# Block-group loads in the second expert pass: issued by ScalarE as two large DMAs instead of eight on SyncE, and gathers begun four rows ahead

## The chip, the cores and the metric

The kernel runs on one core of a Trainium2 chip. Its time is the device time of one execution in microseconds, the median of several runs. A profile is one further execution, taken by the hardware profiler.

## What is computed

The kernel is one step of a decoder layer for 512 prompt tokens and 64 sample tokens (width 2048, float32): a modulated norm, a combined input projection with a recurrent branch and a short convolution, an output projection, and then a layer of many tiny experts. Only this last layer matters here. Every token picks 16 of 16384 experts for each of 8 heads; an expert is one row of `u` and one row of `v`.

```
eidx = ...                                   # (token, head, 16): the experts picked, by product keys
g    = softmax(top)                          # their weights
act  = gelu(einsum('td,thkd->thk', x, u[eidx])) * g
out  = einsum('thk,thkd->td', act, v[eidx])
```

## The kernel before

The experts are 128 blocks of 128 rows. Blocks that are picked often are computed in full for all 512 prompt tokens, as dense matrix products: `L` = 88 of them. What the tokens pick in the other 40 blocks, and all picks of the sample tokens, is gathered row by row. The second half of the kernel is therefore two long passes on TensorE, with gathers woven between.

**The u part** runs over 88 blocks in two halves each (`NU2` = 176 halves, line 1492). `u_half` (line 1253) multiplies a half with the tokens; after the second half ScalarE takes the gelu and stores the block's activations to DRAM (`actd`, line 1267). In the meantime the matrix of weights, by block and token, is built in chunks and stored to DRAM as `gd` (line 1468).

**The v part** runs over `M` = 88 steps. A step takes four blocks (a "group", `SG` = 4, of which there are 22) and a quarter of the 2048 output columns, in four columns of 128 (`kq`, line 1596). `v_column` (line 1271) does 12 matmuls for a column, so a step has 48. Eight blocks, two groups, accumulate in PSUM over two steps; after the second, `v_sum` (line 1300) adds the bank to `acc` in SBUF: by ScalarE for the first eight blocks (line 1303), by VectorE after that (line 1305). Two buffers hold a bank of each kind, so that a late addition stops TensorE.

Both passes split every operand in two for precision. `ahead` (line 881) loads weights into `raw` on SyncE's queue (line 859 for u, 864 for v, two DMAs for each half) and converts them: ScalarE writes `xhi` (line 875), GpSimd `xlo` (line 876). A load waits until `xlo` has been made from the same buffer; a conversion waits until TensorE has used the buffer it writes. There are four buffers in the v part, and conversions run one step ahead.

Each group also needs its activations times its weights, split in two:

- `load_group(sg, j)` (line 1217) loads the group. It is called four times, with j = 0 to 3. Each call issues two DMAs on SyncE: the activations of one block (line 1223, 256 KB) and a quarter of the chunks of the weights `gd` (line 1224, 256 KB in runs of 512 B). The two tiles, `actr` and `gsb`, exist once.
- `weigh(sg)` (line 1227) multiplies them on VectorE, in `actr`'s place.
- `halve(sg, 0)` makes `ahi` on ScalarE (line 1237), `halve(sg, 1)` makes `alo` on VectorE (line 1241). After that `actr` is free for the next group.

When these are emitted is planned ahead: `jobs` (lines 1560 to 1572) maps a column's number (four a step) to calls. With `h_` the column of the first half of the split, and `hi_at` that of the group before, the four loads come at `hi_at + 5` to `hi_at + 8`, `weigh` at `h_ - 4`, the halves at `h_` and `h_ + 2`. The constraints in the loop make `h_` 16 columns, four steps, after `hi_at`. Groups 0 and 1 are loaded in the last 14 halves of the u part (from `E0`, lines 1539 to 1548).

**The gathers.** `gather_u` and `gather_v` (lines 1126 and 1160) append to two lists: `fetches` (an indirect DMA that GpSimd issues, line 1123, 128 rows of up to 8 KB into one row buffer) and `uses` (VectorE: a dot product at line 1151, or `accB += row * dots` at line 1177). `gather_to` (line 1206) walks through the uses in step with the columns, and before each use emits fetches up to a number of rows ahead. In the v part there are `RV` = 6 row buffers and the lead is `RV - 1` rows, the next use among them.

Every engine executes its instructions in the order in which this code emits them, and an instruction that waits for a semaphore holds all behind it.

Of the kernel before, what the change touches and what calls it, by code (L numbers as in the profile page):

```python
# [5 lines left out]
F32 = mybir.dt.float32  # L6
# [22 lines left out]
NA = NP  # L29
# [3 lines left out]
SG = 4  # L33
# [3 lines left out]
TC = 32  # L37
NCH = NA // TC
QT = NA // 128
SORTED = ((0, 64, 36), (64, 128, 43), (192, 128, 33), (320, 128, 27), (448, 64, 10))  # L40
RB = 4
RV = 6
# [32 lines left out]
def build(ctx, tc, A, O, dbg=None):  # L75
    nc = tc.nc
# [328 lines left out]
    o = big.tile([128, KD, T], F32, name="o", tag="big")  # L405

    def project(src, nm):
        his, los = stream_w(src, nm)
        p = pp.tile([128, 2, 512], F32, name=f"pp_{nm}", tag="pp")
        mm3([p[:, 0, :HT], p[:, 1, :HT]], his, los, movs)  # L410
        return p
# [185 lines left out]
    for k in range(KD):  # L597
        p = project(A["w_out"][k], f"o{k}")
# [32 lines left out]
    for q in range(4):  # L631
# [7 lines left out]
        t = adap.tile([128, 4, 512], F32, name=f"h2s{q}", tag="wa")  # L639
# [32 lines left out]
    gd = dr.tile([NCH, 128, L, TC], F32, name="gd")  # L672
    actd = dr.tile([L, 128, NA], F32, name="actd")
# [111 lines left out]
    slot_of, row_log, slots_now = {}, [], [RB]  # L785
# [8 lines left out]
    def row_free():  # L794

        s_ = (slot_of.get(len(row_log) - 1, -1) + 1) % slots_now[0]
        return all(row_log[k] for k in range(max(0, len(row_log) - 2 * RV), len(row_log)) if slot_of[k] == s_)
# [46 lines left out]
    raws, parts, gsb, ahl, acts, pools = {}, {}, {}, {}, {}, {}  # L844
# [36 lines left out]
    def ahead(l, c):  # L881
        while at["l"] <= min(l, len(stream) - 1):
            load(at["l"])
            at["l"] += 1
        while at["c"] <= min(c, len(stream) - 1):
            conv(at["c"])
            at["c"] += 1
# [73 lines left out]
    def sample_twice():  # L961

        for k0 in range(0, KD, 8):
            r, a = new_row(f"dup{k0}")
            row_log[a] = True
            d = r.bitcast(F32R).rearrange("p (q k t) -> p q k t", q=2, t=128)
            dups.append(d)
            for q in range(2):
                S.activation(d[:, q].rearrange("p k (r t) -> p k r t", t=NG),
                             r32(hv[q][:, k0:k0 + 8, None, NA:T]).to_broadcast([128, 8, 2, NG]), AF.Copy)  # L970

    def sample_rows():

        hT = first_h["h"] = psum["p"].tile([128, D], F32, name="hT0", tag="hT", bufs=1)
        for k in range(KD):
            for q in range(2):
                PE.matmul(hT[:, k * 128:(k + 1) * 128], dups[k // 8][:, q, k % 8, :], identr, start=q == 0, stop=q == 1)
# [134 lines left out]
    fetches, uses = [], []  # L1112
# [4 lines left out]
    def flush(n):  # L1117
        while after and after[0][0] <= n:
            after.pop(0)[1]()
# [84 lines left out]
    gf, gu = [0], [0]  # L1204

    def gather_to(n, lim=1 << 30):

        n = min(int(n), lim)
        while gu[0] < min(n, len(uses)):
            while gf[0] < min(len(fetches), gu[0] + (RB if slots_now[0] == RB else RV - 1), lim) and row_free():  # L1210
                fetches[gf[0]]()
                gf[0] += 1
            uses[gu[0]]()
            gu[0] += 1
            flush(gu[0])

    def load_group(sg, j):

        if j == 0:
            gsb[sg] = ep.tile([128, NCH, SG * TC], F32, name=f"gsb{sg}", tag="gsb", bufs=1)  # L1220
            acts[sg] = ep.tile([128, SG, NA], F32, name=f"actr{sg}", tag="actr", bufs=1)
        c = slice(j * NCH // 4, (j + 1) * NCH // 4)
        nc.sync.dma_start(acts[sg][:, j, :], actd[SG * sg + j])  # L1223
        nc.sync.dma_start(gsb[sg][:, c, :].rearrange("p c (i t) -> p c i t", t=TC),
                          gd[c, :, sg * SG:(sg + 1) * SG, :].rearrange("c p i t -> p c i t"))

    def weigh(sg):

        a = acts[sg].rearrange("p i (c t) -> p i c t", t=TC)
        V.tensor_tensor(a, a, gsb.pop(sg).rearrange("p c (i t) -> p i c t", t=TC), op=ALU.mult)  # L1230
# [195 lines left out]
    def g_start():  # L1426

        kb = pbank("g", "kb", 2)
        S.activation(kb[:, :L], perm[:, :L], AF.Copy)
        S.activation(kb[:, L:L + 128], iota, AF.Copy)  # L1430
        gk["w"], gk["o"] = kb[:, :L], kb[:, L:L + 128]
        gk["g"] = pbank("g", "gbank", 2)

    def g_pair(b):

        rg = pools["rg"]
        t0 = b * 4
        ops = rg.tile([128, 8, 128], F32, name=f"op{b}", tag="op", bufs=PAIRS // 2)
        wr = rg.tile([128, 8, L], F32, name=f"wr{b}", tag="wr", bufs=PAIRS // 2)
        for out, src, j in ((ops, gk["o"], 1), (wr, gk["w"], 0)):  # L1440
            n = src.shape[-1]
            V.tensor_tensor(out, src[:, None, :].to_broadcast([128, 8, n]),  # L1442
                            it[j][:, t0:t0 + 8, None].to_broadcast([128, 8, n]), op=ALU.is_equal)
        pair[b], pair[b + 1] = (ops, wr, 0), (ops, wr, 4)

    def g_scale(b):

        ops, wr, j0 = pair[b]
        for j in range(4):
            S.activation(ops[:, j0 + j, :], ops[:, j0 + j, :], AF.Copy, scale=it[2][:, b * 4 + j:b * 4 + j + 1])  # L1450
# [19 lines left out]
    def put(n):  # L1470
        for f in puts[:n]:
            f()
        del puts[:n]

    E0 = NU2 - 14
# [4 lines left out]
    ep = None  # L1480

    def upto(n):
        return min(NB2, max(0, (n - R1) * NB2 // (E0 - 6 - R1)))

    def g_one(n):
        nonlocal spare
        if gm[1] < min(upto(n - LAG), gm[2]):
            g_out(gm[1], g_mm(gm[1]))
            gm[1] += 1
            spare += 0.4  # L1490

    for n in range(NU2):
        _, i, c = stream[n]
        if n == 0:
            sample_twice()
        if n == 1:
            sample_rows()
        ahead(n + 3, n + 2)
        spare += PIECE
        if R1 is not None:  # L1500
            if not gk:
                g_start()
            put(2)
            g_one(n)
            if gm[0] < min(upto(n), gm[1] + PAIRS - 1):
                g_pair(gm[0])
                gm[0] += 2
                spare -= 2.2
            while gm[2] < min(gm[0], gm[1] + PAIRS - 2):
                g_scale(gm[2])  # L1510
                gm[2] += 1

        if R2 is None:
            due_g += RATE[R1 is not None] if ready[0] else 0
            g0 = gu[0]
            gather_to(due_g, ready[0])
            due_g = min(due_g, gu[0] + 1.0)
            spare -= 2.4 * (gu[0] - g0)
        else:
            gather_to(G0 + (NU + EARLY_V - G0) * (n + 1 - R2) // (NU2 - R2))  # L1520
        while spare > 0 and R2 is None:
            cost = next(steps1 if R1 is None else steps2, "end")
            if cost == "end":
                if R1 is None:
                    R1 = n
                else:
                    R2, G0 = n, gu[0]
                break
            if cost is None:
                break  # L1530
            spare -= cost
        if n == E0:
            assert not pair and not stg
            put(len(puts))
            p2.close()
            epx = ctx.enter_context(ExitStack())
            ep = epx.enter_context(tc.tile_pool(name="ep", bufs=1))
        u_half(n, i, c)
        for sg, o in ((0, 1), (1, 7)):
            if n - E0 in (o, o + 1):  # L1540
                load_group(sg, 2 * (n - E0 - o))
                load_group(sg, 2 * (n - E0 - o) + 1)
            if n - E0 == o + 3:
                weigh(sg)
            if n - E0 == o + 4:
                halve(sg, 0)
            if n - E0 == o + 5:
                halve(sg, 1)
    hp_.close()
    vp = ctx.enter_context(tc.tile_pool(name="vp", bufs=1, side="right"))  # L1550
# [9 lines left out]
    jobs = {}  # L1560
    hi_at = -4
    for sg in range(2, L // SG):
        use = uses_of[sg * SG]
        free = KQ * (uses_of[(sg - 3) * SG][-1] + 1) if sg >= 3 else 0
        h_ = min(KQ * use[0] - 7, max(free, hi_at + 16))
        assert h_ >= free and h_ >= hi_at + 13, (sg, h_, free, hi_at)
        for j in range(4):
            jobs.setdefault(hi_at + 5 + j, []).append(lambda sg=sg, j=j: load_group(sg, j))
        jobs.setdefault(h_ - 4, []).append(lambda sg=sg: weigh(sg))
        jobs.setdefault(h_, []).append(lambda sg=sg: halve(sg, 0))  # L1570
        jobs.setdefault(h_ + 2, []).append(lambda sg=sg: halve(sg, 1))
        hi_at = h_
# [8 lines left out]
    for m in range(M):  # L1581
        gi, q, bl, first, final = steps[m]
        n = NU2 + 2 * m
# [186 lines left out]
```

## Time and profile before

| | us |
|---|---|
| Median of 3 runs | 3539.17 (3532.54 to 3542.3) |
| Profiled execution, its own time | 3548.6 |
| Span of the profile | 3546.7 |
| PE (TensorE matmul) busy | 3291.2 |
| DVE (VectorE) busy | 2225.9 |
| POOL (GpSimd) busy | 1784.3 |
| ACT (ScalarE) busy | 1114.5 |

Busy times are of one profiled execution; matmuls are pipelined, so a busy PE isn't PE at its peak. SP is SyncE, which only issues DMAs here. PEld is the weight load of TensorE. An engine's name with a q is its sequencer, which waits and issues. q0 is the DMA queue of GpSimd's gathers, q1 that of SyncE, q10 that of ScalarE. In a group of instructions the idle time is that of the engine just before them, and what follows the arrow ended most of it; the profile infers this from semaphores. Times within the execution count from the span's start. The last halves of the u part lie at 2280 to 2381 us, the v part's steps from 2381 to about 3519 us.

### The profile page before, as it was taken

The numbers are of one execution on the slowest core, as the hardware profiler recorded it, in microseconds if no ns is written. First come the engines' busy times: TensorE is split into PE (matmuls) and PEld (weight loads), VectorE is DVE, ScalarE is ACT, GpSimd is POOL, SyncE is SP. The second block draws the span as 40 slices with busy tenths as digits, with TensorE's granted clock in tenths as the row PEclk, the third lists the DMA queues.
The fourth block names the chain that finished last, engine by engine and source line by source line (L and its number), as shares of the span: only waits on it lengthen the run. The fifth ranks groups of instructions, "written<-read, shape, count | busy, mean of one in ns | idle before, by whom it ended". The sixth has DMA issues, their size and how long they took to land. (4 is left out here: it accounts for less than half of the span.)

```text
span 3546.7 us, 48881 instructions
## 1 busy us (share of the span) xinstructions
PE 3291.2 (93%) x18023; PEld 2786.2 (79%) x18023; DVE 2225.9 (63%) x3370; ACT 1114.5 (31%) x1692; POOL 1784.3 (50%) x1017
## 2 busy tenths in 40 slices
PE   5899999989889999999999999979888999798996
PEld 2688788889789988788888888857776778587775
DVE  5356322253448979787877777765666666575745
ACT  3244211132232232255555555322122222222222
POOL 4233233344333346565655666666665666566542
PEclk8899999999989999999999999989999999899998
DMA  9643566624422238699879998899989787888844
GB/s 336 227 141 129 173 212 208 212 91 130 147 92 72 78 117 297 223 345 355 313 250 352 343 381 356 328 369 365 344 297 342 240 290 251 292 298 275 299 149 154
DMA packets 313910, 875.70 MB, mean 247 GB/s; under 512 B 40560, under 2 KB 86960, under 8 KB 266192
## 3 DMA queue, kind: packets, MB, share of 16 engines
q1 hardware_dynamic: 228176, 445.09, 37.4%
q0 software_dynamic: 63600, 381.29, 28.0%
q10 hardware_dynamic: 21888, 46.15, 3.3%
q8 instruction: 142, 2.33, 0.3%
q14 instruction: 104, 0.85, 0.1%
HBM read 879.50 MB, written 71.07 MB: 268 GB/s over the span
## 5 line engine op out<-in xcount | busy, mean ns | idle before, releaser
L876 POOL TENSOR_TENSOR xlo<-raw,xhi 128x1024 fp32r<-128x1024 f32 x352 | 861.1, 2458 | 601.5 <-ACT xhi L875 593.8
L875 ACT ACTIVATE xhi<-raw 128x1024 fp32r<-128x1024 f32 x352 | 371.0, 1059 | 945.8 <-PE pv L1283 398.2
L1283 PE MATMUL pv<-ahi,xhi 128*128 128x512 f32 x1408 | 569.4, 404 | 81.0 <-DVE acc L1305 73.7
L1151 DVE SCALAR_TENSOR_TENSOR u<-u,hT 128x2048 f32<-128x2048 f32 x213 | 483.0, 2283 | 172.2 <-DMA u<-u,rows 157.5
L1263 PE MATMUL pu<-hhi,xhi 128*128 128x512 f32 x1408 | 567.4, 403 | 14.8 <-ACT xhi L875 14.8
L1283 PE MATMUL pv<-ahi,xlo 128*128 128x512 f32 x1408 | 564.7, 401 | 15.2 <-POOL xlo L876 15.2
L1283 PE MATMUL pv<-alo,xhi 128*128 128x512 f32 x1408 | 562.5, 400 | 0.0
L1263 PE MATMUL pu<-hhi,xlo 128*128 128x512 f32 x1408 | 554.7, 394 | 5.1 <-POOL xlo L876 5.0
L1263 PE MATMUL pu<-hlo,xhi 128*128 128x512 f32 x1408 | 556.4, 395 | 0.0
L1177 DVE SCALAR_TENSOR_TENSOR accB<-v,dots,accB 128x2048 f32<-128x2048 f32 x207 | 486.7, 2351 | 47.5 <-DMA v<-v,rows 44.4
L1283 PEld LDWEIGHTS pv<-ahi,xhi 128*128 128x128 f32 x1408 | 271.6, 193 | 146.5 <-issue 64.5
L1123 POOL DMA_INDIRECT v<-v,rows x213 | 243.8, 1145 | 182.4 <-DVE accB L1177 88.2
L1283 PEld LDWEIGHTS pv<-ahi,xlo 128*128 128x128 f32 x1408 | 271.4, 193 | 81.5 <-POOL xlo L876 17.5
L1263 PEld LDWEIGHTS pu<-hhi,xhi 128*128 128x128 f32 x1408 | 267.5, 190 | 70.6 <-ACT xhi L875 15.7
L1283 PEld LDWEIGHTS pv<-alo,xhi 128*128 128x128 f32 x1408 | 271.9, 193 | 61.7
L1263 PEld LDWEIGHTS pu<-hhi,xlo 128*128 128x128 f32 x1408 | 266.4, 189 | 67.3 <-POOL xlo L876 7.8
L1263 PEld LDWEIGHTS pu<-hlo,xhi 128*128 128x128 f32 x1408 | 267.5, 190 | 52.7
L1123 POOL DMA_INDIRECT u<-u,rows x213 | 217.1, 1019 | 101.2 <-DVE u L1151 60.5
L1230 DVE TENSOR_TENSOR actr<-actr,gsb 128x2048 f32<-128x2048 f32 x22 | 60.8, 2763 | 215.7 <-DMA gsb<-gd 149.6
L1305 DVE TENSOR_TENSOR acc<-acc,pv 128x512 f32<-128x512 f32 x160 | 107.6, 682 | 113.3 <-PE pv L1283 109.1
L1450 ACT ACTIVATE op<-op,it 128x128 f32<-128x128 f32 x512 | 155.3, 388 | 44.4 <-DVE op L1442 44.4
L184 PE MATMUL ada<-wa,cpad 128*32 128x512 f32 x768 | 115.3, 706 | 41.3 <-DMA wa<-w_ada 41.3
(471 smaller groups left out, 5670.4 us busy)
## 6 DMA issues: line engine op xcount, KB each, us to landing
wa<-w_ada SPq DMA_DIRECT2D x96, 1024.0 KB
raw<-ut SPq DMA_DIRECT2D x176, 512.0 KB
raw<-v SPq DMA_DIRECT2D x352, 256.0 KB
actd<-act ACTq DMA_DIRECT2D x88, 256.0 KB
gd<-stg ACTq DMA_DIRECT2D x64, 352.0 KB
actr<-actd SPq DMA_DIRECT2D x88, 256.0 KB
gsb<-gd SPq DMA_DIRECT2D x88, 256.0 KB
raw_o<-w_out SPq DMA_DIRECT2D x32, 512.0 KB
```

Source lines behind the costliest of these rows:

```text
L184: PE.matmul(acc[32 * g:32 * g + 32, :], cpad[:, 4 * kq + g, :], w[:, g, :], start=kq == 0, stop=kq == 3)
L875: S.activation(hi, raw, AF.Copy)
L876: G.tensor_sub(lo, raw, r32(hi))
L1123: G.indirect_dma_start(out=out, out_offset=None, in_=src, in_offset=bass.IndirectOffsetOnAxis(ap=idx, axis=0), bounds_check=NE * 128 - 1, ...
L1151: V.scalar_tensor_tensor(r, r, 1.0, st["h"], op0=ALU.mult, op1=ALU.mult, accum_out=dots[i][:, j:j + 1])
L1177: V.scalar_tensor_tensor(st["a"], r, dots[i][:, j:j + 1], st["a"], op0=ALU.mult, op1=ALU.add)
L1230: V.tensor_tensor(a, a, gsb.pop(sg).rearrange("p c (i t) -> p i c t", t=TC), op=ALU.mult)
L1263: PE.matmul(pu, st[:, kk, :], movA[mv](k), start=k == 0 and a == 0, stop=k == KD - 1 and a == 2)
L1283: PE.matmul(pv, st, mv, start=first and j == 0 and a == 0, stop=last and not end and j == SG - 1 and a == 2)
L1305: V.tensor_add(ak, ak, pv)
L1450: S.activation(ops[:, j0 + j, :], ops[:, j0 + j, :], AF.Copy, scale=it[2][:, b * 4 + j:b * 4 + j + 1])
```

## The change

Three things change, all around the v part:

- `load_group` has two calls for each group instead of four, each with one DMA, issued by ScalarE: j = 0 loads all four blocks' activations (1 MB, runs of 2 KB), j = 1 all of the group's weights (1 MB, runs of 512 B).
- The plan: the weights' load comes first, at `hi_at + 2` (or 9 columns ahead of `weigh` where two groups lie more than 20 columns apart, which the plan above doesn't give), the activations' at `hi_at + 5`. For group 0, in the u part, the activations are loaded first, and `weigh` and the split come one half later; for group 1 the weights are loaded first.
- `gather_to` begins rows `RV - 2` = 4 ahead in the v part instead of 5; the row buffers stay at six.

```diff
@@ gather_to
-            while gf[0] < min(len(fetches), gu[0] + (RB if slots_now[0] == RB else RV - 1), lim) and row_free():
+            while gf[0] < min(len(fetches), gu[0] + (RB if slots_now[0] == RB else RV - 2), lim) and row_free():
@@ load_group
         if j == 0:
+            acts[sg] = ep.tile([128, SG, NA], F32, name=f"actr{sg}", tag="actr", bufs=1)
+            nc.scalar.dma_start(acts[sg], actd[SG * sg:SG * sg + SG].rearrange("i p t -> p i t"))
+        else:
             gsb[sg] = ep.tile([128, NCH, SG * TC], F32, name=f"gsb{sg}", tag="gsb", bufs=1)
-            acts[sg] = ep.tile([128, SG, NA], F32, name=f"actr{sg}", tag="actr", bufs=1)
-        c = slice(j * NCH // 4, (j + 1) * NCH // 4)
-        nc.sync.dma_start(acts[sg][:, j, :], actd[SG * sg + j])
-        nc.sync.dma_start(gsb[sg][:, c, :].rearrange("p c (i t) -> p c i t", t=TC),
-                          gd[c, :, sg * SG:(sg + 1) * SG, :].rearrange("c p i t -> p c i t"))
+            nc.scalar.dma_start(gsb[sg], gd[:, :, sg * SG:(sg + 1) * SG, :].rearrange("c p i t -> p c (i t)"))
@@ the u part's last halves
-        for sg, o in ((0, 1), (1, 7)):
+        for sg, o, first in ((0, 1, 0), (1, 7, 1)):
             if n - E0 in (o, o + 1):
-                load_group(sg, 2 * (n - E0 - o))
-                load_group(sg, 2 * (n - E0 - o) + 1)
-            if n - E0 == o + 3:
+                load_group(sg, first ^ (n - E0 - o))
+            if n - E0 == o + 4 - sg:
                 weigh(sg)
-            if n - E0 == o + 4:
+            if n - E0 == o + 5 - sg:
                 halve(sg, 0)
-            if n - E0 == o + 5:
+            if n - E0 == o + 6 - sg:
                 halve(sg, 1)
@@ the v part's plan
-        for j in range(4):
-            jobs.setdefault(hi_at + 5 + j, []).append(lambda sg=sg, j=j: load_group(sg, j))
+        for t_, j in ((h_ - 4 - 9 if h_ - hi_at > 20 else hi_at + 2, 1), (hi_at + 5, 0)):
+            jobs.setdefault(max(t_, 0), []).append(lambda sg=sg, j=j: load_group(sg, j))
```

## The prediction

> **What bounds the kernel now.** I read the page's costliest groups first, for what TensorE waits on in the v part, then the chain of work that ended last, the windows by stage, and the timelines of SP, VectorE and ScalarE around one block group. In the groups the columns are line, engine, operation, tiles, count | busy us, mean ns | idle us before, and what ended it.
>
> ```profile
> span 3546.7 us, 48881 instructions
> ...
> L1283 PE MATMUL pv<-ahi,xhi 128*128 128x512 f32 x1408 | 569.4, 404 | 81.0 <-DVE acc L1305 73.7
> ...
> L1177 DVE SCALAR_TENSOR_TENSOR accB<-v,dots,accB 128x2048 f32<-128x2048 f32 x207 | 486.7, 2351 | 47.5 <-DMA v<-v,rows 44.4
> L1123 POOL DMA_INDIRECT v<-v,rows x213 | 243.8, 1145 | 182.4 <-DVE accB L1177 88.2
> L1283 PEld LDWEIGHTS pv<-ahi,xlo 128*128 128x128 f32 x1408 | 271.4, 193 | 81.5 <-POOL xlo L876 17.5
> ...
> L1230 DVE TENSOR_TENSOR actr<-actr,gsb 128x2048 f32<-128x2048 f32 x22 | 60.8, 2763 | 215.7 <-DMA gsb<-gd 149.6
> ```
>
> TensorE's own waits in the v part come to 81.0 us, and 73.7 us of them end when VectorE finishes an addition at L1305, which frees a PSUM bank. VectorE is late because `weigh` (L1230) is: 22 of them work 60.8 us and wait 215.7 us, mostly for `gsb`. The chain shows how one such wait becomes TensorE's (start, us, what):
>
> ```profile
> 2495.86 18.93 DMA actr<-actd
> ...
> 2515.65 13.29 DMA gsb<-gd
> ...
> 2533.04 2.35 DVE accB L1177
> ...
> 2895.46 135.30 PE pv L1283 x576
> ```
>
> Two loads in a row, 32.2 us, then the row sums queued behind `weigh`, then TensorE. The last row is a stretch without a stall: 576 matmuls, twelve steps of 48, in 135.3 us, so a step is 11.3 us. Now the stages (length, then busy time of PE, PEld, DVE, ACT and POOL, then granted clock, DMA share, GB/s):
>
> ```profile
> 2280.00:2381.00 101.00, 81.06 (x321) 63.58 (x320) 67.86 (x37) 20.93 (x23) 59.88 (x38) 0.88 0.92 349
> 2425.00:3381.00 956.00, 863.33 (x3629) 696.19 (x3628) 638.93 (x372) 210.39 (x193) 589.50 (x342) 0.95 0.83 294
> 2911.00:3017.00 106.00, 106.00 (x462) 86.31 (x461) 72.15 (x46) 22.71 (x20) 72.08 (x42) 1.00 0.74 254
> ```
>
> The v part without its first four steps (2425 to 3381) has 92.7 us without a matmul and a clock of 0.95; where nothing stalls the clock is 1.00. So stalls cost twice: up to 0.05 x 863.3 = 43 us go in slower matmuls beside them. The end of the u part, where groups 0 and 1 are loaded, has 19.9 us idle and a clock of 0.88, some 10 us more.
>
> **The change part by part.** First, why the loads are late, in one group's timeline of SP:
>
> ```profile
> 2489.27 5.59 SPq L864 DMA_DIRECT2D raw<-v  x4
> 2494.95 0.38 SPq L1223 DMA_DIRECT2D actr<-actd  x1
> 2495.38 0.42 SPq L1224 DMA_DIRECT2D gsb<-gd  x1
> ...
> 2497.77 6.79 SPq L1223 DMA_DIRECT2D actr<-actd  x1
> 2504.60 2.60 SPq L1224 DMA_DIRECT2D gsb<-gd  x1
> 2507.78 6.82 SPq L864 DMA_DIRECT2D raw<-v  x4
> 2514.81 0.33 SPq L1223 DMA_DIRECT2D actr<-actd  x1
> 2515.65 0.38 SPq L1224 DMA_DIRECT2D gsb<-gd  x1
> ```
>
> The first piece goes out at 2494.95, behind weight loads that wait for their buffers; an issue of 0.4 us becomes 6.79 us when much is queued already; the fourth piece, a step later in the program, stands behind four more weight loads and goes at 2515.65. The same group on VectorE and ScalarE:
>
> ```profile
> 2487.61 3.79 DVE L1241 TENSOR_TENSOR alo<-actr,ahi 128x2048 fp32r<-128x2048 f32 x1
> ...
> 2508.06 2.35 DVE L1177 SCALAR_TENSOR_TENSOR accB<-v,dots,accB 128x2048 f32<-128x2048 f32 x1
> 2529.03 4.09 DVE L1230 TENSOR_TENSOR actr<-actr,gsb 128x2048 f32<-128x2048 f32 x1 [18.62 <-DMA gsb<-gd]
> ```
>
> ```profile
> 2480.16 1.07 ACT L1303 ACTIVATE acc<-pv 128x512 f32<-128x512 f32 x2
> ...
> 2485.71 2.00 ACT L875 ACTIVATE xhi<-raw 128x1024 fp32r<-128x1024 f32 x2
> 2494.70 1.06 ACT L875 ACTIVATE xhi<-raw 128x1024 fp32r<-128x1024 f32 x1 [6.99 <-PE pv L1283]
> ```
>
> VectorE wants the group at 2510.4. In the changed program `gsb` is issued two columns after the first half of the split, which on ScalarE is at 2481.2, 34 us before the old last piece; the buffer's reader, the `weigh` before, is then long done. The activations follow three columns later, after the conversions that end at 2487.7; their buffer is read until 2491.4 (`alo`). So ScalarE gains a wait of 3.7 us; behind it stands the conversion of 2494.70, which waits for TensorE anyway, so the wait is hidden. If VectorE is 4 us later than here, the conversion is late, then `xlo`, then TensorE.
>
> Does 2 MB land by 2510.4? The queues' packets, first in a stretch with rows in flight (3076 to 3082), then in one without (3084 to 3089), then over the stage:
>
> ```profile
> q0 software_dynamic: 308, 2.26, 91.4%
> q1 hardware_dynamic: 310, 0.20, 11.1%
> ...
> q1 hardware_dynamic: 1425, 1.84, 107.7%
> ...
> q0 software_dynamic: 27189, 158.47, 43.7%
> q1 hardware_dynamic: 96249, 121.41, 38.8%
> ```
>
> Beside gathers a queue gets one packet for each of theirs: 310 in 6 us, 52 a us. Alone it gets 1425 in 5 us, 285 a us. `gsb` is 2048 runs of 512 B and the activations 512 of 2 KB: 2560 packets in the 29.2 us from 2481.2, 88 a us. With q0 active 43.7% of the stage the mean is 0.437 x 52 + 0.563 x 285 = 183 a us for one queue beside it; weights on q1 take turns too, so I take half, 92, just enough. The ends are 2560/285 = 9 us and 2560/52 = 49 us. A miss of a few us is covered, as VectorE is busy 638.9 of 956 us. The Trainium skill, page "DMA: Bandwidth & Descriptors", section "Queues, rings and completion order", says that an engine takes a packet of some 9 to 17 descriptors from a ring before it switches; by it 2048 short runs would need a ninth of the turns or less, and the loads could not be late (rival 2 would fall away, the sum would rise to its upper end). The trace has 310 against 308, one for one; the measurement decides.
>
> So the **sum**, against the profiled execution's 3548.6 us (its span of 3546.7 and 1.9 around it):
> - VectorE's lateness: of 73.7 us I take three quarters, 55 (ends 0 and 73.7). The waits for `xlo` (17.5 in the weight loads' row) I leave; POOL's scatters hold some of them.
> - The clock: 43 us times 55/92.7, that is 26 (ends 0 and 43).
> - End of the u part: 19.9 + 10, of which half, 15; there SP no longer holds weight loads behind the group, but ScalarE's stores of activations now queue behind 2048 packets (ends -20, if ScalarE is held where SP was, and 30). That `weigh` and the split of group 0 move by one half of a u block costs nothing: the first v step reads them, seven halves after the split.
> - Gathers one row less ahead: -5. Of 213 rows 20 are used before the v part; the planned 84 steps use 193/84 = 2.3 each, one every 4.9 us; a fetch is issued 4.9 us nearer to its use. The nearest row of a bare fetch:
>
> ```profile
> 3048.25 1.03 POOL L1123 DMA_INDIRECT v<-v,rows  x1 [0.30 <-PE pv L1283]
> ...
> 3055.95 2.36 DVE L1177 SCALAR_TENSOR_TENSOR accB<-v,dots,accB 128x2048 f32<-128x2048 f32 x1 [6.07 <-DMA v<-v,rows]
> ```
>
>   It landed 7.7 us after its issue, and three or four rows of lead are 15 to 20 us, so few more rows are late. Ends: 44.4 us of VectorE waits doubled, which its idle third hides but for some 20; and a gain of 10, as GpSimd's 88.2 us behind `accB` shrink, because the slot's last use is one row further back.
> - ScalarE: 44 issues, 0.3 to 0.6 us each, beside 210 busy of 956: nothing; 176 issues leave SP. For a hold at the activations' issue: -7 (ends 0, and rival 3), most of it for group 2, whose two loads go out together in the first v step.
>
> ```profile
> 3439.54 0.63 SPq L1357 DMA_DIRECT2D y<-x2b  x1
> 3440.22 2.89 SPq L1294 DMA_DIRECT2D xf<-x1d  x1
> ```
>
>   `y<-x2b` is also 2048 runs (of 256 B): its own issue took 0.63 us, and the next DMA of that queue was held 2.89 us. On ScalarE the next DMA comes a step later, with most of `gsb` gone.
>
> 55 + 26 + 15 - 5 - 7 = 84: 3464.6 us profiled. The profiled execution lies 9.4 us over the median of 3539.17, so **3455 us**; with VectorE's term at a half or in full, and the clock with it, the sum is 27 less or 27 more, and with the u part's end as far off again its own range is 3410 to 3500.
>
> **The rivals.**
> 1. *Forecast*, 0.66.
> 2. *The loads still land late*: on a third queue the short packets get one turn in three, 35 a us or so beside gathers and weights (310 x 2/3 in 6 us), 2560 in 73 us at worst. For: DMA share 0.83, 0.92 at the end of the u part. Against: they start 34 us earlier, and q0 is quiet over half the time. Half of 84: 3497. Chance 0.16.
> 3. *Slower: ScalarE is held by its own issue.* Place: the `gsb` issue, where conversions, hence `xlo` and TensorE, queue behind it. If an issue lasts until half its packets have drained, 1024 take 4 us at 285 and 20 us at 52. The next conversion is due within a step, some 10 us later; a hold of 16 us stalls the twenty later groups 6 us each, 120 us on top of the forecast: 3455 + 120 = 3575. It decides from a hold of about 14 us, where 20 stalls of 4.2 us take back the 84. Against: 0.63 us for 2048 runs above; and the ring of one issuer doesn't hold the other:
>
> ```profile
> 2286.19 3.88 SPq L859 DMA_DIRECT2D raw<-ut  x1
> ...
> 2287.66 0.33 ACTq L1267 DMA_DIRECT2D actd<-act  x1
> ```
>
>    The Trainium skill, page "Perfetto Trace Analysis", section "DMA Instruction — HWDGE (DVE, Sync)", states this rule: the issuer is free only when all descriptors are generated, on a generator locked for one user at a time. By it the change would give this rival's time; the two pairs of rows speak against both halves. Chance 0.12.
> 4. *Nothing*: another wait takes the place, most likely rows (44.4 us) or weights, since the stage's share of the gain, 81 us, at the same bytes means 294 x 956/875 = 321 GB/s, while 349 were seen at the end of the u part. 3535. Chance 0.06.
>
> **How the numbers follow.** A measurement of this kernel can tell about 0.3% (10.6 us) from no change. Faster by more: cases 1 and 2, 0.82. Within: case 4, 0.06. Slower: case 3, 0.12. The range, 3405 to 3545, takes in cases 1, 2 and 4 but for 0.06 at the lower edge, and leaves out case 3: 0.18 outside. Its lower end is the sum with 73.7, 43 and 17 of the 30 us.
>
> **What would show it.** Right: L1230's 215.7 us of waits fall below 70, L1283's 73.7 below 25, the stage's clock rises to 0.98, SP's issues keep to 0.3 us, and ScalarE's two issues a group stay below 1 us. Wrong: ScalarE issues of 5 us and more with `xlo` ending TensorE's waits (rival 3); L1230 still waiting for `gsb` (rival 2); L1177 waiting over 100 us for rows (the lookahead). The u part's end is the term I know least.

## The result, and the profile after

The changed kernel takes **3449.53 us** (median of 4 runs, 3448.71 to 3457.65); the kernel before, run beside it, 3540.74 (3532.54 to 3546.73). The ratio is 0.9749, with a 95% interval of 0.9724 to 0.9774: 2.5% faster. The profiled execution took 3450.2 us, 98.4 less than the one of before. Ratios, here and below, are of the fast executions: two slow ones, 5834.89 us in run 1 and 11283.89 us of the kernel before beside runs 9 and 10, are left out.

The rows of the page that answer to those of before; `load_group` has become one line shorter, so lines behind it count one lower (L1229 is `weigh`, L1282 the v part's matmul, L1302 and L1304 the additions):

```profile
span 3448.3 us, 48660 instructions
...
L1177 DVE SCALAR_TENSOR_TENSOR accB<-v,dots,accB 128x2048 f32<-128x2048 f32 x207 | 486.8, 2352 | 138.8 <-DMA v<-v,rows 136.3
...
L1282 PE MATMUL pv<-ahi,xhi 128*128 128x512 f32 x1408 | 560.4, 398 | 8.3 <-DVE acc L1304 4.7
...
L1282 PEld LDWEIGHTS pv<-ahi,xlo 128*128 128x128 f32 x1408 | 266.9, 190 | 78.0 <-POOL xlo L876 16.2
...
L1123 POOL DMA_INDIRECT v<-v,rows x213 | 247.9, 1164 | 65.9 <-issue 28.9
```

The group of `weigh`, from the groups of VectorE:

```profile
L1229 DVE TENSOR_TENSOR actr<-actr,gsb 128x2048 f32<-128x2048 f32 x22 | 70.9, 3224 | 26.8 <-DMA actr<-actd 18.1 <-DMA raw<-v 8.7
```

TensorE's waits for VectorE's addition fell from 73.7 to 4.7 us, `weigh`'s waits from 215.7 to 26.8. The waits for gathered rows tripled, from 44.4 to 136.3 us, and the kernel is faster all the same. GpSimd's wait before a gather, 182.4 us, is 65.9 now.

The windows by stage (length, busy time of PE, PEld, DVE, ACT and POOL, granted clock, DMA share, GB/s): the end of the u part, and steps 4 to 79 of the v part, for the changed kernel and then for the one before.

```profile
2280.00:2381.00 101.00, 82.83 (x327) 64.25 (x325) 70.65 (x40) 21.98 (x24) 61.69 (x40) 0.92 0.96 362
...
2432.50:3292.50 860.00, 846.87 (x3650) 686.50 (x3649) 622.91 (x372) 212.00 (x192) 590.30 (x342) 1.00 0.89 324
```

```profile
2438.70:3391.90 953.20, 867.82 (x3649) 700.16 (x3650) 639.46 (x374) 212.50 (x195) 587.81 (x343) 0.95 0.82 291
```

Same matmuls, 93.2 us less: 72.3 us of it is time without a matmul (85.4 before, 13.1 now) and 20.9 us is faster matmuls. From the starts of the matmuls the 98.4 us of the span divide so: end of the u part 3.5, steps 0 to 3 2.7, steps 4 to 79 93.2, the rest -1.0. Three pieces of the chain of waits in the changed kernel:

```profile
2298.56 15.39 ACTq L1266
...
2408.96 189.76 PE pv L1282 x814
...
2614.74 337.88 PE pv L1282 x1458
```

The longest stretch without a stall was 576 matmuls before; now 1458 run in a row (30 steps, 11.1 us each). And the first row is new: a store of activations on ScalarE's queue in the u part, held for 15.39 us.

What has become of the group that the prediction showed on SyncE: from the timeline of ScalarE, and from that of VectorE (start, us, what, and the wait ahead of it).

```profile
2472.07 0.37 ACTq L1224 DMA_DIRECT2D gsb<-gd  x1
2472.87 1.90 ACT L1236 ACTIVATE ahi<-actr 128x2048 fp32r<-128x2048 f32 x1
...
2477.72 0.78 ACTq L1221 DMA_DIRECT2D actr<-actd  x1
```

```profile
2509.62 2.29 DVE L1229 TENSOR_TENSOR actr<-actr,gsb 128x2048 f32<-128x2048 f32 x1 [4.84 <-DMA actr<-actd]
```

The last piece went out at 2515.65 before; now the second of the two loads is issued at 2477.72, and `weigh` waits 4.84 us instead of 18.62. Of its 26.8 us of waits, 18.8 belong to groups 1 to 4; the 17 groups after that wait 8 us between them.

### The profile page after: what moved, and what is told of

Read it like the earlier page. It is cut to its first block, busy times and chain, and to the rows that moved or that the text cites. A ratio compares the mean times of both kernels' runs of the same rounds, so it can differ in the third digit from the quotient of the medians.

```text
span 3448.3 us, 48660 instructions
## 1 busy us (share of the span) xinstructions
PE 3274.8 (95%) x18023; PEld 2774.9 (80%) x18023; DVE 2220.5 (64%) x3370; ACT 1114.0 (32%) x1692; POOL 1788.7 (52%) x1017
## 4 chain that ended last, share of the span: by engine, by line
PE 55%; DMA 6%; DVE 5%; issue 3%; POOL 2%; ACT 0%; ACTq 0%; SPq 0%; POOLq 0%; DVEq 0%
PE pv L1282 23%; PE pu L1262 20%; PE qa L134 3%; PE wide L134 3%; PE gbank L1455 3%; DMA v<-v,rows 2%; DVE u L1151 1%; DMA gsb<-gd 1%; DMA u<-u,rows 1%; DMA raw<-v 1%; DVE flags L992 1%; POOL xlo L876 1%; POOL v L1123 0%; PE sc L708 0%; ACTq L1266 0%
## 5 line engine op out<-in xcount | busy, mean ns | idle before, releaser
L1177 DVE SCALAR_TENSOR_TENSOR accB<-v,dots,accB 128x2048 f32<-128x2048 f32 x207 | 486.8, 2352 | 138.8 <-DMA v<-v,rows 136.3
L1282 PE MATMUL pv<-ahi,xlo 128*128 128x512 f32 x1408 | 559.6, 397 | 11.7 <-POOL xlo L876 11.7
L1282 PE MATMUL pv<-ahi,xhi 128*128 128x512 f32 x1408 | 560.4, 398 | 8.3 <-DVE acc L1304 4.7
L1282 PE MATMUL pv<-alo,xhi 128*128 128x512 f32 x1408 | 555.5, 395 | 0.0
L1282 PEld LDWEIGHTS pv<-ahi,xlo 128*128 128x128 f32 x1408 | 266.9, 190 | 78.0 <-POOL xlo L876 16.2
L1282 PEld LDWEIGHTS pv<-ahi,xhi 128*128 128x128 f32 x1408 | 267.2, 190 | 68.8 <-DVE acc L1304 4.0
L1262 PEld LDWEIGHTS pu<-hhi,xhi 128*128 128x128 f32 x1408 | 267.3, 190 | 66.2 <-ACT xhi L875 11.1
L1282 PEld LDWEIGHTS pv<-alo,xhi 128*128 128x128 f32 x1408 | 267.1, 190 | 60.8
L1123 POOL DMA_INDIRECT v<-v,rows x213 | 247.9, 1164 | 65.9 <-issue 28.9
L1304 DVE TENSOR_TENSOR acc<-acc,pv 128x512 f32<-128x512 f32 x160 | 107.5, 682 | 114.9 <-PE pv L1282 114.7
L1455 PEld LDWEIGHTS gbank<-wr,op 128*128 128x128 f32 x1024 | 134.0, 191 | 15.7 <-ACT stg L1462 5.0
```

What stands on the lines that cost most here:

```text
L1123: G.indirect_dma_start(out=out, out_offset=None, in_=src, in_offset=bass.IndirectOffsetOnAxis(ap=idx, axis=0), bounds_check=NE * 128 - 1, ...
L1177: V.scalar_tensor_tensor(st["a"], r, dots[i][:, j:j + 1], st["a"], op0=ALU.mult, op1=ALU.add)
L1262: PE.matmul(pu, st[:, kk, :], movA[mv](k), start=k == 0 and a == 0, stop=k == KD - 1 and a == 2)
L1282: PE.matmul(pv, st, mv, start=first and j == 0 and a == 0, stop=last and not end and j == SG - 1 and a == 2)
L1304: V.tensor_add(ak, ak, pv)
L1455: PE.matmul(pg[:, j * L:(j + 1) * L], ops[:, j0 + j, :], wr[:, j0 + j, :], start=True, stop=True)
```

## The experiments

The change mixes three things in the loads (the issuing engine, two DMAs for eight, an earlier place in the plan) and a fourth in the gathers. Theory at the outset: the engine matters, since on SyncE an early load would stand behind weight loads or hold them. Rival: the place does it all. Ratios are to the kernel before, with 95% intervals.

**1. Rows five ahead again, in the changed kernel.**

```diff
-  ... (RB if slots_now[0] == RB else RV - 2) ...
+  ... (RB if slots_now[0] == RB else RV - 1) ...
```

> The changed kernel with the gathers' lead back at five rows. Theory (the gain comes from the group loads alone; the shorter lead is close to neutral): VectorE's waits for gathered rows fall from 136.3 us to about 60, GpSimd's waits for accB at L1123 rise from 21.4 us to some 40, TensorE loses nothing by either, and the time stays at 3440 to 3457 us. Rival (the shorter lead carries part of the gain, because it keeps GpSimd from standing behind VectorE): 3465 us or more, with xlo ending 20 us or more of TensorE's waits.

Measured: 3447.8 us, 0.9754 (0.9739 to 0.9770), the same as the changed kernel.

```profile
L1177 DVE SCALAR_TENSOR_TENSOR accB<-v,dots,accB 128x2048 f32<-128x2048 f32 x207 | 486.9, 2352 | 57.2 <-DMA v<-v,rows 54.6
```

The page's group of the row sums: their waits fall from 136.3 to 54.6 us, and nothing comes of it. In the changed kernel VectorE works 622.9 of the 860 us and waits in time that it has. GpSimd waits 22.9 us for `accB` here and 21.4 with four ahead, so the buffer wasn't the hindrance either, once VectorE was on time.

**2. Rows four ahead alone, in the kernel before.**

```diff
-  ... (RB if slots_now[0] == RB else RV - 1) ...
+  ... (RB if slots_now[0] == RB else RV - 2) ...
```

> The kernel before with nothing changed but the gathers' lead, four rows. Theory: the weigh of L1230 still waits some 200 us for its loads, so at most GpSimd's 88.2 us behind accB shrink: 3525 to 3545 us. Rival (the lead carries part): 3515 us or less.

Measured: 3518.51 us, 0.9956 (0.9938 to 0.9975), between the two. In the old plan a shorter lead does help, by 0.4%; the page's group of the gathers:

```profile
L1123 POOL DMA_INDIRECT v<-v,rows x213 | 246.6, 1158 | 93.9 <-DVE accB L1177 50.5
```

GpSimd waits 50.5 us for `accB` instead of 88.2, and TensorE 54.4 us for VectorE's addition instead of 73.7. Probably a GpSimd that stands behind a late VectorE makes `xlo` and rows late in turn. In the changed kernel that gain has already been had: the two don't add up.

**3. The new plan with both loads on SyncE.**

```diff
-            nc.scalar.dma_start(acts[sg], ...)
+            nc.sync.dma_start(acts[sg], ...)
...
-            nc.scalar.dma_start(gsb[sg], ...)
+            nc.sync.dma_start(gsb[sg], ...)
```

> The changed kernel with its two group loads issued by SyncE at the new places. Theory (both the early place and the queue of its own count): the loads now stand behind weight loads, and weight loads behind 2048 packets of 512 B; the weigh waits less than before (below 80 us), but the conversions wait for weights over 150 us, and the time is 3475 to 3515 us. Rival (the place in the plan does it all): 3445 to 3460 us. Rival (the queue does it all): 3530 us or more.

Measured: 3451.74 us, 0.9767 (0.9749 to 0.9786). The theory fell: SyncE does as well. It was right about the holds (conversions wait 177.9 us for weights, 76.9 in the changed kernel), not about their price. The issues of the v part's weight loads (minimum, median and longest in ns), in this run and then in the changed kernel:

```profile
L864 SPq DMA_DIRECT2D raw<-v x352: 332/333/12663, 2350.6 to 3355.9; - x176
```

```profile
L864 SPq DMA_DIRECT2D raw<-v x352: 332/333/2503, 2351.1 to 3358.5; - x176
```

An issue behind the big load is held up to 12.7 us, but `raw` runs far enough ahead that TensorE's matmuls wait only 9.7 us for `xlo` in the v part, against 11.7 in the changed kernel. The Trainium skill, page "DMA: Bandwidth & Descriptors", section "Issuing engines are not separate DMA queues", says that issuing on several engines saves only the sequencer's time of issue, since all share the same 16 DMA engines; at the new places the runs agree (0.9767 against 0.9749), and so they do at the old places with two DMAs (runs 5 and 10, 0.9901 and 0.9894). With eight pieces at the old places they don't, as the next run shows.

**4. The eight pieces at their old places, issued by ScalarE.**

```diff
-        nc.sync.dma_start(acts[sg][:, j, :], actd[SG * sg + j])
-        nc.sync.dma_start(gsb[sg][:, c, :] ...)
+        nc.scalar.dma_start(acts[sg][:, j, :], actd[SG * sg + j])
+        nc.scalar.dma_start(gsb[sg][:, c, :] ...)
```

> The kernel before with its eight pieces for each group issued by ScalarE at their old places. Theory (a DMA is held while the one before it on its queue has packets to place): of the eight issues several are held for 5 to 15 us on ScalarE, the conversions stand behind them, xlo comes late and TensorE waits for it 50 us or more; but the pieces go out earlier than on SyncE: 3490 to 3560 us. Rival (issues on ScalarE are never held for long): every issue below 1 us and 3470 us or less.

Measured: 3472.52 us, 0.9814 (0.9792 to 0.9835). Again a miss, on the other side: the engine alone, with nothing moved and nothing merged, gives 63.5 us. The longest of the eight issues took 6.88 us, and TensorE waited 17.6 us for `xlo`, not 50. `weigh` in the groups of VectorE:

```profile
L1230 DVE TENSOR_TENSOR actr<-actr,gsb 128x2048 f32<-128x2048 f32 x22 | 58.5, 2660 | 131.7 <-DMA gsb<-gd 85.0 <-DMA raw<-v 46.8
```

`weigh` still waits 131.7 us, and TensorE 20.6 us for VectorE. So engine and place each give most of the gain alone, and together no more than the place. That asked for a common cause: perhaps when the last piece goes out.

**5. Two merged DMAs on SyncE at the old places.**

```diff
+            acts[sg] = ep.tile(...)
+            nc.sync.dma_start(acts[sg], actd[SG * sg:SG * sg + SG].rearrange("i p t -> p i t"))
+        else:
+            gsb[sg] = ep.tile(...)
+            nc.sync.dma_start(gsb[sg], gd[:, :, sg * SG:(sg + 1) * SG, :].rearrange("c p i t -> p c (i t)"))
@@ the u part's last halves
-                load_group(sg, 2 * (n - E0 - o))
-                load_group(sg, 2 * (n - E0 - o) + 1)
+                load_group(sg, n - E0 - o)
@@ plan
-        for j in range(4):
+        for j in range(2):
             jobs.setdefault(hi_at + 5 + j, []).append(...)
```

> The kernel before with the eight pieces merged into two DMAs, issued by SyncE at the old places: the activations where their first piece stood, the gradient weights one job later, where the second pieces stood; rows still five ahead, weighing where it was. Of the kernel before the last quarter of the gradient weights was issued 10 to 26 us after the first one, and its last packets landed 0.5 to 0.9 us ahead of the weighing in 18 of 22 groups. Theory (what counts is when the last of the eight quarters goes out, against a weighing that the plan holds in place): the merged DMA goes out 10 to 18 us ahead of the old last quarter, so most of the lateness goes: 3450 to 3475 us, VectorE's waits at the weighing below 110 us (216 before). Rival (the earlier place in the plan is what counts, and merging alone does little): 3490 to 3530 us, with the waits above 150 us.

Measured: 3499.39 us, 0.9901 (0.9886 to 0.9916). The time is in the rival's range, the waits just under its 150 us: merging takes `weigh`'s waits from 215.7 to 146.5 us only, all of them now for `gsb` (groups of VectorE):

```profile
L1229 DVE TENSOR_TENSOR actr<-actr,gsb 128x2048 f32<-128x2048 f32 x22 | 59.0, 2683 | 146.5 <-DMA gsb<-gd 146.5
```

**6. Eight pieces on SyncE at the new places**: the changed kernel with engine and merging undone.

```diff
-            nc.scalar.dma_start(acts[sg], ...)
+            for i in range(SG):
+                nc.sync.dma_start(acts[sg][:, i, :], actd[SG * sg + i])
...
-            nc.scalar.dma_start(gsb[sg], ...)
+            for i in range(4):
+                c = slice(i * NCH // 4, (i + 1) * NCH // 4)
+                nc.sync.dma_start(gsb[sg][:, c, :] ..., gd[c, ...] ...)
```

> The changed kernel with its two DMAs cut into the eight old pieces again (four of 8 x 512-byte lines and four of 8 KB lines), all issued by SyncE, four at once at each of the two new places. Theory (when the last quarter goes out is what counts): four quarters in one burst go out within 5 to 15 us at the new place, still 5 us or more ahead of the weighing: 3450 to 3475 us, VectorE's waits at the weighing below 100 us. Rival (eight issues on SyncE hold back the block weights' own loads behind them, whatever the place): 3490 to 3530 us, with TensorE stalled on the halves of the weights (xlo, xhi) for more than 40 us.

Measured: 3447.05 us, 0.9754 (0.9739 to 0.9769): all of the gain, with neither ScalarE nor large DMAs, and a little under the theory's range; the rival's stalls didn't come (TensorE waits 11.1 us for `xlo` in the v part). `weigh` in the groups of VectorE:

```profile
L1233 DVE TENSOR_TENSOR actr<-actr,gsb 128x2048 f32<-128x2048 f32 x22 | 65.0, 2954 | 68.1 <-DMA actr<-actd 68.1
```

One group in the timeline of SyncE, and its `weigh` in that of VectorE:

```profile
2469.40 8.86 SPq L1227 DMA_DIRECT2D gsb<-gd  x4
2478.84 4.97 SPq L864 DMA_DIRECT2D raw<-v  x4
2483.91 1.91 SPq L1222 DMA_DIRECT2D actr<-actd  x4
```

```profile
2502.74 2.29 DVE L1233 TENSOR_TENSOR actr<-actr,gsb 128x2048 f32<-128x2048 f32 x1 [4.21 <-DMA actr<-actd]
```

The four quarters are issued in 8.86 us, and all eight pieces are out at 2485.8, 12.7 us before VectorE is free for `weigh` (2502.74 less its wait of 4.21). In the kernel before the last piece went out 5.2 us after that point (2515.65 against 2510.4). The new places also send the pieces in two bursts of four instead of four pairs; this run doesn't part the two, run 10 against run 1 does.

**7. The u part's stores on SyncE.** The changed kernel holds two stores behind a group's loads. One is the first row of its chain above; the other, in its timeline of ScalarE:

```profile
2345.25 0.38 ACTq L1221 DMA_DIRECT2D actr<-actd  x1
...
2346.72 0.58 ACT L1265 ACTIVATE act<-pu 128x512 f32<-128x512 f32 x1
2347.33 13.59 ACTq L1266 DMA_DIRECT2D actd<-act  x1
2361.02 2.00 ACT L875 ACTIVATE xhi<-raw 128x1024 fp32r<-128x1024 f32 x2 [13.72 <-issue]
```

```diff
-            nc.scalar.dma_start(actd[i], act)
+            (nc.sync if n >= E0 else nc.scalar).dma_start(actd[i], act)
```

> The changed kernel with the stores of the activations in the last 14 halves of the u part issued by SyncE instead of ScalarE, so that they don't stand behind the gradient weights' load on ScalarE's queue, where two of them were held 15.4 and 13.6 us and TensorE stalled 6.4 and 4.2 us with a slower stretch after each. Theory (these holds are what the u part's end still costs): the v part begins 8 to 14 us earlier and the time is 3436 to 3445 us. Rival (SyncE, which issues in order, waits for each GELU and sends the next weights late, so that the stall only changes its place): 3448 to 3460 us, with SyncE's wait at the store above 10 us each time.

Measured: 3452.58 us, 0.9770 (0.9756 to 0.9785). No gain: the rival's time came, and its sign (SyncE waits 87.0 us for seven stores), but the stall came by another road than it named. No store is held on ScalarE any more; now `gsb` of group 0 lands late, why isn't shown, and ScalarE waits for VectorE (timelines of ScalarE and of VectorE):

```profile
2336.58 1.91 ACT L1236 ACTIVATE ahi<-actr 128x2048 fp32r<-128x2048 f32 x1 [19.99 <-DVE actr L1229]
```

```profile
2334.25 2.29 DVE L1229 TENSOR_TENSOR actr<-actr,gsb 128x2048 f32<-128x2048 f32 x1 [12.85 <-DMA gsb<-gd]
```

The split stands ahead of the next conversion on ScalarE, and TensorE stalls 12.1 us for `xhi`, once, instead of 6.2 and 4.0.

**8. The same with rows five ahead.**

> The run above, with rows begun five ahead again. If the lead of the rows doesn't matter in the changed kernel, the same as the run above within 0.15%. If it had hidden behind the holds in the u part: 5 to 10 us less than the run above. It is the version that by the theory beats both kernels: 3434 to 3445 us.

Measured: 3451.36 us, 0.9747 (0.9730 to 0.9764), as the run above within the intervals, and not the theory's 3434 to 3445: the lead doesn't matter here either, and the place of the stores doesn't.

**9. Groups 0 and 1 on SyncE, group 2 with its activations first**, to have the u part's end of run 5 with the rest of run 1 (rows five ahead).

```diff
-            nc.scalar.dma_start(acts[sg], ...)
+            (nc.sync if sg < 2 else nc.scalar).dma_start(acts[sg], ...)
-            nc.scalar.dma_start(gsb[sg], ...)
+            (nc.sync if sg < 2 else nc.scalar).dma_start(gsb[sg], ...)
@@ the u part's last halves: activations first, weighing as before the change
-                load_group(sg, first ^ (n - E0 - o))
+                load_group(sg, n - E0 - o)
@@ plan
-        for t_, j in ((... hi_at + 2, 1), (hi_at + 5, 0)):
+        for t_, j in ((... hi_at + 2, sg > 2), (hi_at + 5, sg == 2)):
```

> The changed kernel with rows five ahead, in which groups 0 and 1 are loaded by SyncE (two DMAs at the places and with the weighings of the run that merged them at the old places), group 2 by ScalarE with its activations ahead of its gradient weights, and all later groups as in the changed kernel. Two traces point to it: with the u part's loads on SyncE at the old places the v part began at 2367.7 us, in the changed kernel at 2377.1 (2375.8 with rows five ahead); and group 2's activations, second on ScalarE's queue, were held 14.9 us there, after which steps 1 and 2 took 6.0 us more than the 11.07 us of a steady step. Theory (both add): 9 us earlier into the v part and 4 to 6 us less in steps 1 and 2: 3432 to 3440 us. Rival (what is gained at the u part's end is lost at the next thing that is late there, as with the stores on SyncE): 3444 to 3452 us, with the v part beginning at 2374 or later.

Measured: 3453.53 us, 0.9776 (0.9755 to 0.9796). The rival held (the v part began at 2378.8; the time is just over its range). The hold only changed its victim: a weight load for the u part now stands behind `gsb`, and ScalarE's conversion waits for it: the timeline of SyncE, and TensorE's waits (us, times, longest).

```profile
2338.47 0.68 SPq L1224 DMA_DIRECT2D gsb<-gd  x1
2339.72 16.88 SPq L859 DMA_DIRECT2D raw<-ut  x1
```

```profile
PE pu L1262 <- ACT xhi L875: 12.5, 2, 9.9
```

The expectation also read run 5 wrongly. Its v part began 9.4 us earlier than the changed kernel's, but its last 14 u halves did so too, at 2268.6 instead of 2275.7 us: 7.1 of the 9.4 us lay ahead of the part that it compared. Counted from there to their last matmul, these halves took 104.5 us before, 101.1 in the changed kernel, 98.8 in run 5 and 103.0 in this one; the shortest are 96.1 in run 4 and 97.9 in run 6. No version of the first groups' loads made the whole kernel measurably faster than the changed one.

**10. Two merged DMAs on ScalarE at the old places.**

```diff
@@ run 5
-            nc.sync.dma_start(acts[sg], ...)
+            nc.scalar.dma_start(acts[sg], ...)
-            nc.sync.dma_start(gsb[sg], ...)
+            nc.scalar.dma_start(gsb[sg], ...)
```

> The kernel before with the two merged DMAs at the old places, as in the run that merged them there, but issued by ScalarE: the last of the eight combinations of engine, pieces and place. Theory (the place decides, since the gradient weights land no sooner from another engine): within 0.6% of that run, 3480 to 3515 us, and the steps of the v part take 60 us or more over 11.07 us each. Rival (ScalarE's queue is worth 1 to 2% at the old places, as the eight pieces showed): 3455 to 3475 us, with less than 50 us over.

Measured: 3498.72 us, 0.9894 (0.9868 to 0.9921), as run 5; the theory held. It is the cleanest pair for the place: run 1 has the same engine, the same two DMAs and the same lead, and differs by the plan alone (with it the order of a group's two loads and the treatment of the first two groups); its ratio is 0.9754. The group of `weigh`, and one group in the timelines of ScalarE and VectorE:

```profile
L1229 DVE TENSOR_TENSOR actr<-actr,gsb 128x2048 f32<-128x2048 f32 x22 | 65.3, 2969 | 162.1 <-DMA gsb<-gd 162.1
```

```profile
2491.01 0.37 ACTq L1221 DMA_DIRECT2D actr<-actd  x1
2491.41 0.52 ACTq L1224 DMA_DIRECT2D gsb<-gd  x1
```

```profile
2526.63 2.29 DVE L1229 TENSOR_TENSOR actr<-actr,gsb 128x2048 f32<-128x2048 f32 x1 [18.26 <-DMA gsb<-gd]
2528.84 2.35 DVE L1177 SCALAR_TENSOR_TENSOR accB<-v,dots,accB 128x2048 f32<-128x2048 f32 x1
```

These issues aren't held, and `weigh` still waits 18.26 us: both loads are issued at 2491, and the 2 MB take until 2526. The transfer isn't slower than in the changed kernel, where the same group took 37.6 us from its first issue to `weigh` (35.6 here). It begins later: `gsb` is issued 17.0 us ahead of the point where VectorE is free for `weigh` (2508.37), in the changed kernel 32.7 us ahead (2472.07 against 2504.78).

Seven of the eight combinations, with the waits of `weigh`, TensorE's waits for VectorE's addition, and length and clock of steps 4 to 79 (us):

| engine, DMAs, place | ratio | `weigh` waits | TensorE waits | steps 4-79 | clock |
|---|---|---|---|---|---|
| SyncE, 8, old (before) | 1 | 215.7 | 73.7 | 953.2 | 0.95 |
| ScalarE, 2, old (run 10) | 0.9894 | 162.1 | 40.1 | 919.9 | 0.96 |
| SyncE, 2, old (run 5) | 0.9901 | 146.5 | 33.1 | 903.8 | 0.97 |
| ScalarE, 8, old (run 4) | 0.9814 | 131.7 | 20.6 | 889.8 | 0.98 |
| SyncE, 2, new (run 3) | 0.9767 | 71.1 | 4.3 | 861.6 | 0.99 |
| SyncE, 8, new (run 6) | 0.9754 | 68.1 | 4.3 | 860.4 | 0.99 |
| ScalarE, 2, new (changed) | 0.9749 | 26.8 | 4.7 | 860.0 | 1.00 |

The columns behind the ratio are of one profiled execution each, and runs 4 and 5 are nearer in them (3484.98 and 3486.89 us) than in their medians (3472.52 and 3499.39). Down the table waits and lengths fall together (runs 10 and 5 are equal within their intervals, and so are the last three rows): `weigh`'s lateness, then TensorE's, then the time. From 71.1 us down `weigh`'s waits cost TensorE nothing more. How far ahead of the need a load begins goes roughly with the table. On the mean of groups 3 to 20, in the traces, the first issue of `gsb` lies ahead of the point where VectorE is free for `weigh` (its start less its wait) by 18.3 us before, 16.9 in run 5, 22.0 in run 10, 23.1 in run 4, 28.2 and 28.3 in runs 3 and 6, and 35.3 in the changed kernel. The last issue alone doesn't order the runs: it lies 0.4 us behind that point before, but 10.1 ahead in run 4 and 21.4 ahead in run 10, and run 10 has the longer waits.

Rows four ahead go with the new places but for run 1; by runs 1 and 2 that explains 0.4% at most. Why eight pieces do better than two on ScalarE at the old places (0.9814 against 0.9894) is open: the traces show `weigh` waiting less, not why.

## Why the prediction was right, point by point

Forecast 3455 us, measured 3449.53. The chain was read rightly: late loads, late `weigh`, late additions, TensorE's stalls, slower matmuls. The terms:

- **VectorE's lateness**, 55 of 73.7 taken: 69.0 went (73.7 to 4.7). The quarter left over as a precaution wasn't needed. Of the rest of the 72.3 us of idle time, 3.5 are waits for `xlo` (15.2 to 11.7 before matmuls).
- **The clock**, 26: 20.9 us, from the busy time of the same matmuls.
- **The end of the u part**, 15: 3.5. This is the term that was mis-sized, within its ends of -20 and 30. The clock rose as foreseen (0.88 to 0.92), but TensorE is idle 18.2 us there instead of 19.9. What the prediction named against it came, ScalarE's stores behind 2048 packets: 15.39 and 13.59 us of holds, and TensorE's stalls for `xhi` of 6.2 and 4.0 us stand in place of two of before that took 14.8. Runs 7 and 9, which moved the stores and the loads, did not get the gain either; run 4 got 8.4 us and run 6 6.6 (104.5 less 96.1 and 97.9).
- **Gathers one row less ahead**, -5: nothing measurable. The row waits rose by 91.9 us, further than the term's end had it (doubled), and VectorE's spare time hid all of it (run 1). The sign that the prediction gave for this being wrong, L1177 waiting over 100 us, came (138.8) and meant nothing: a wait on an engine with over a quarter of its time free has no price of its own.
- **ScalarE's holds**, -7: right in size at the place that it named. `gsb` is never held (0.37 to 0.51 us in 22 issues); the activations' issue behind it is, 0.37 to 14.87 us with a median of 0.93. Group 2, the one named, has the longest:

```profile
2389.94 0.38 ACTq L1224 DMA_DIRECT2D gsb<-gd  x1
2390.36 14.87 ACTq L1221 DMA_DIRECT2D actr<-actd  x1
2405.40 2.00 ACT L875 ACTIVATE xhi<-raw 128x1024 fp32r<-128x1024 f32 x2 [14.42 <-DMA raw<-v]
2407.31 1.07 ACT L1302 ACTIVATE acc<-pv 128x512 f32<-128x512 f32 x2
```

  The addition at 2407.31 was due when TensorE needed its bank; steps 1 and 2 together took 6.0 us more than two steady steps. The four first steps still gained 2.7 us, since stalls of before went there too. The later holds stand ahead of conversions that wait for TensorE anyway, as the prediction had it.
- **The packets**: a load of 2 MB was put at 92 a us. In the group shown, 2560 packets take 37.5 us to the start of `weigh`, 68 a us or a little more: within the ends, and just late enough for the wait of 4.84 us. The issue is earlier than worked out, by the mean of groups 3 to 20 35.3 us ahead of the need and not 29.2, so that two errors partly cancel; runs 3 and 6, with 28.2 and 28.3 us, suggest that with the issue as worked out the time would have been the same.
- **The stage and the range**: the window called the v part without its first four steps, 2425 to 3381, begins before step 4 does (2438.7); with steps 4 to 79 proper the idle time is 85.4 us, not 92.7. The sum's own range of 3410 to 3500 doesn't follow from its terms: 27 either way and as much again would be 3401 to 3509. And 3405 comes out of 73.7, 43 and 17 only without the -5 and -7.

The sum of 84 met 98.4 us of the profiled executions: 17.3 more of idle time in steps 4 to 79 (72.3 against 55), 5.1 less from the clock, 11.5 less at the u part's end, 5 more from the gathers, 9.7 more in the first steps (2.7 against -7), and 1.0 less in the rest. Errors of 32.0 one way met 17.6 the other, so that part of the nearness of the total is luck.

Of the rivals, 3 had its mechanism half right: holds of 15 us exist, but they fall on the next DMA of the queue, where the plan leaves three columns between. Rival 2 did not come: 26.8 us of waits are left. Rival 4's reason, more bytes a second than the stage had shown, did not bind: it moves 324 GB/s now, as worked out (321).

What the prediction had for certain and the runs did not bear out is that ScalarE has a part in it. It priced the change as made; which of its parts does the work it did not ask. The place does (run 6 against before: 0.9754; run 1 against run 10: 0.9754 against 0.9894); engine and merging help only as long as the place is late. No version beat the changed kernel: runs 1, 6 and 8 are equal to it within their intervals.

## What to carry to other kernels

When a load lands late, look first at when its issues go out against when its reader is due and how long the transfer takes (here 36 to 38 us for a group's 2 MB in the two groups shown), and move the issue; a queue of its own and larger DMAs are other ways to the same few microseconds, and what they give doesn't add. A hold behind a large DMA of short runs doesn't go away by giving it to another engine: leave a stretch in that queue behind it in which nothing urgent stands. Price a wait only by what waits behind it: 92 us more of row waits on VectorE cost nothing, and 15 us at one place of ScalarE cost 6.

## What the runs showed of the hardware

**The issue of 2048 short runs is short; the next DMA pays.** In the changed kernel `gsb` (2048 runs of 512 B) is issued by ScalarE in 0.37 to 0.51 us, and the following DMA of that queue took up to 15.4 us; on SyncE the same load held the following one up to 17.2 us (u weight loads, runs 3 and 9) and 20.9 us (v weight loads, run 5). The Trainium skill, page "Perfetto Trace Analysis", section "DMA Instruction — HWDGE (DVE, Sync)", has the issuer itself wait until the descriptors are generated, on a generator for one user at a time; here the issuer is free after 0.37 to 0.51 us and the next DMA pays, and during ScalarE's hold of 14.87 us at 2390.36 SyncE issued four weight loads in 0.33 us each.

**A stall of a few us is followed by slow matmuls.** TensorE in the changed kernel, around a stall of 4.50 us:

```profile
2609.85 0.39 PE L1282 MATMUL pv<-alo,xhi 128*128 128x512 f32 x1
2614.74 0.79 PE L1282 MATMUL pv<-ahi,xlo 128*128 128x512 f32 x1 [4.50 <-POOL xlo L876]
2615.33 0.63 PE L1282 MATMUL pv<-ahi,xhi 128*128 128x512 f32 x1
```

Matmuls take 0.39 us ahead of it. Behind it come one of 0.79, five of 0.63 and one of 0.56 us, begun about 0.43 us after one another instead of 0.23; from the eighth on, 3.1 us after the first, it is 0.39 again. This step takes 17.25 us where the median is 11.08: 4.7 us for the late start and 1.5 for the slow matmuls. In run 7 the stall of 12.09 us is followed by two slow matmuls, a further wait of 1.81 us and eight more. Over steps 4 to 79 a us of TensorE's waiting for VectorE went with (953.2 - 860.0) / (73.7 - 4.7) = 1.35 us of time; 3.3 of the 93.2 us are other idle time.
